# A delta-net inverse by substitution in blocks of four and two doublings, and product groups two steps apart

## The chip, the cores and the metric

The kernel runs on one core of a Trainium2 chip. The metric is the device time of one execution in microseconds (us), and lower is better. The engines are named as in the profile: PE is the matmul engine (PEld its weight loads, which overlap the matmuls), DVE the vector engine, ACT the scalar engine, POOL GpSimd, and SP the queue that issues most DMAs. L12 is line 12 of the kernel's file.

## The reference

One decoder layer runs on 512 prompt tokens and on 64 sample tokens (8 sequences of 8), 576 columns in all, with a model width of 2048. The layer is a normalisation, an input projection, eight gated delta-net heads beside four mLSTM heads, an output projection with a residual, and a convolutional FFN of width 5632. Everything is fp32. The part that the change touches is the solve in a delta-net head:

```python
lower = jnp.where(strict, jnp.einsum('nbhik,nbhjk->nbhij', kb, k) * decay, 0.0)
a_mat = lower + jnp.eye(c, dtype=lower.dtype)
solve = functools.partial(lax.linalg.triangular_solve, left_side=True, lower=True, unit_diagonal=True)
u = solve(a_mat, v * beta[..., None])
w = solve(a_mat, kb * jnp.exp(G)[..., None])
```

followed by a scan over chunks that carries a 128x128 state per head. For every chunk a unit triangular matrix has to be inverted, or something equal to it.

## The kernel before

**Dense work.** The large products (input projection, output projection, FFN) are done as three fp32r matmuls for each fp32 one: a weight tile is cut into a high and a low part (ACT makes the high part at L120, DVE the low part at L121), and so is the activation. `three` (L198) issues the six matmuls of one 128x128 weight tile, three kinds by two column halves of 288. I call these six a *step*. After each step `tick` (L170) runs the jobs that are due.

**Jobs.** A head is a Python generator, and `yield n` puts its next piece n steps later. So PE's order is written out by hand: dense steps, and between them the small products of the heads, in groups, where the yields put them. PE is the only engine with a hand-made order (`manual_schedule`, L274). For DVE, ACT, POOL and SP a scheduler makes the order from dependences and priorities, at build time. On the chip each engine runs its list in order; an instruction that waits holds back all behind it.

**PSUM.** The dense products use two buffers called `pd`; all small products take one of four buffers called `pr` in turn (`psr`, L111). A product that takes a buffer waits until the last reader of the product that had it four groups earlier is done.

**A delta-net head** (`dn_head`), 128 keys by 128 values, works on four chunks of 128 prompt tokens and one block of 64 sample tokens. Its groups on PE, in order: L608 (four transposes of k), the sample's products (L614 to L616), whose results feed the short DVE chain L619 to L628 that makes the scale factors `cj`; L635 (k by k, scaled on DVE by L638 into the matrix U); L646 (k by q, scaled by L647); L657 and L662 (transposes of v). Each yield between these groups is one step. Then come the inverse's own groups, the state chain over four chunks (L676, L683, L687, L690; L693 makes the new state on DVE), the sample's products as a job of their own (`dn_sample`, L747 to L771, with L774 on DVE updating the sample states), and a last normalisation over the head's output (L256). The next heads are computed beside this, so the late groups of one head stand among the early groups of the next.

**The inverse** (`inverse`) of a 128x128 unit triangular U starts with its 16x16 diagonal blocks. POOL masks them out, DVE folds them (L797 to L799) into `cb`, and two DMAs through DRAM (`ud`, L803 and L807) put the 40 blocks of a head on 40 partitions, each with its 256 elements along the free axis in the first part of the buffer T. DVE then negates (L809), sets the diagonal (L810) and does a back substitution in 14 pairs of an outer product (L815) and a subtraction (L817). Two DMAs (`xd`, L818, and `cx`, L821) bring the blocks back; L834 spreads them into a block-diagonal X and L836 transposes it into T. From there matmuls double the block size three times (16 to 32, 64, 128), beginning with L843; YI = 8 and YJ = 20 steps lie between the stages, in which the DMAs and the DVE chain run. The 28 instructions L815 and L817 and the DMA L818 have a higher priority (PQ = 1000) in the scheduler.

Of the kernel before, what the change touches and what calls it, by code (L numbers as in the profile page):

```python
# [11 lines left out]
ALU = mybir.AluOpType  # L12
# [20 lines left out]
SB = 16  # L33
# [35 lines left out]
class Layer:  # L69
# [515 lines left out]
    def dn_head(self, h, q, k, v, sz):  # L585
        nc, I, O = self.nc, self.I, self.O
        V, A, Pl, mm = nc.vector, nc.scalar, nc.gpsimd, nc.tensor.matmul
# [18 lines left out]
        for c in range(NCH):  # L606
            sl, n = self.blk(c)
            nc.tensor.transpose(pk[:, sl], k[:, sl], self.ident)  # L608
        for c in range(NCH):
            sl, n = self.blk(c)  # L610
# [15 lines left out]
        U, KQ = self.r(), em  # L626
        V.scalar_tensor_tensor(out=U[0:64, sl4], in0=pk[0:64, P:P + 64], scalar=cjc(4), in1=em[0:64, sl4], op0=ALU.mult, op1=ALU.mult)
        V.tensor_tensor(out=KQ[0:64, sl4], in0=pk[0:64, P + 64:2 * P], in1=em[0:64, sl4], op=ALU.mult)  # L628
        yield 1


        pr = self.psr()
        for c in range(NCH):
            sl, n = self.blk(c)
            mm(pr[:, sl], k[:, sl], k[:, sl], start=True, stop=True)  # L635
        for c in range(NCH):
            sl, n = self.blk(c)
# [1 line left out]
        res = []  # L639
        inv = self.inverse(U, res, YZ if h == 0 else 0)  # L640
        next(inv)
        yield 1
        pr = self.psr()
        for c in range(NCH):
            sl, n = self.blk(c)
            mm(pr[:, sl], k[:, sl], q[:, sl], start=True, stop=True)  # L646
        V.tensor_tensor(out=KQ[:, 0:SEQ], in0=pr, in1=em[:, 0:SEQ], op=ALU.mult)  # L647
        A.activation(q[:, 0:NT], q[:, 0:NT], AF.Square, scale=float(np.sqrt(EPS * P)))
        yield 1


        vs = self.r()
# [2 lines left out]
        for c in range(NCH):  # L655
            sl, n = self.blk(c)
            nc.tensor.transpose(pv[:, sl], v[:, sl], self.ident)  # L657
        for c in range(NCH):
            sl, n = self.blk(c)
# [7 lines left out]
        X, Xs = res  # L667
# [4 lines left out]
        for c in range(NCH):  # L672
            sl, n = self.blk(c)
# [24 lines left out]
            yield W  # L698
        self.later(4, O["pS"][h], S)
        while not sample[3]:  # L700
            yield 1


        ob, sq2 = qe, q[:, 0:NT]
        sq, rs_o, a, u = kd, vs, KQ, X
# [72 lines left out]
    def inverse(self, U, res, more):  # L778
# [3 lines left out]
        V, A, Pl, mm = nc.vector, nc.scalar, nc.gpsimd, nc.tensor.matmul  # L782
        c4 = lambda t: t[:, 0:SEQ].rearrange("p (c i) -> p c i", c=NCH)
        blocks = lambda t, n: t.rearrange("p (c b i) -> p c b i", c=n, i=SB)
        X, T = self.r(), self.r()
        d = lane = T
        Xs = self.t1([64, 64], "Xs", 2)
        nb = P // SB
# [5 lines left out]
        for t, o in ((blocks(d[:, 0:SEQ], NCH), cb[:, 0:4]), (blocks(d[0:64, SEQ:NT], 1), cb[0:64, 4:5])):  # L794
            n = t.shape[2]
            while n > 2:
# [4 lines left out]
        rows = lambda t: t.rearrange("c b r i -> (b r) c i")  # L801
        lanes = lambda t: t.rearrange("c b r i -> (c b) r i")
        nc.sync.dma_start(out=rows(ud), in_=cb)  # L803
        u, x = (lane[0:5 * nb, SB * SB * i:SB * SB * i + SB * SB].rearrange("p (r i) -> p r i", i=SB)
                for i in range(2))
        w = lane[0:5 * nb, 2 * SB * SB:2 * SB * SB + 4 * SB]
        nc.sync.dma_start(out=u, in_=lanes(ud))  # L807
        yield YI
        V.tensor_scalar(out=x, in0=u, scalar1=-1.0, scalar2=None, op0=ALU.mult)  # L809
        V.memset(lane[0:5 * nb, SB * SB:2 * SB * SB:SB + 1], 1.0)  # L810
        self.tc.cur_priority -= PQ
        for j in range(SB - 2, 0, -1):
            n = SB - 1 - j
            wv = w[:, 0:j * n].rearrange("p (r i) -> p r i", r=j)
            V.tensor_tensor(out=wv, in0=u[:, 0:j, j:j + 1].to_broadcast([5 * nb, j, n]),  # L815
                            in1=x[:, j:j + 1, j + 1:].to_broadcast([5 * nb, j, n]), op=ALU.mult)
            V.tensor_tensor(out=x[:, 0:j, j + 1:], in0=x[:, 0:j, j + 1:], in1=wv, op=ALU.subtract)  # L817
        nc.sync.dma_start(out=lanes(xd), in_=x)  # L818
        self.tc.cur_priority += PQ
        cx = self.t1([P, 5, SB], "cx", 2)  # L820
# [10 lines left out]
        for t, c, k in ((blocks(X[:, 0:SEQ], NCH), cx[:, 0:4], P), (blocks(Xs, 1), cx[0:64, 4:5], 64)):  # L831
            n = k // SB
            shape = list(t.shape)
            V.tensor_tensor(out=t, in0=c.unsqueeze(2).to_broadcast(shape),  # L834
                            in1=self.con[0:k, C_RB:C_RB + n].unsqueeze(1).unsqueeze(3).to_broadcast(shape), op=ALU.mult)
# [38 lines left out]
        for a in range(2):  # L874
            x = Xv[64 * a:64 * a + 32, :, 64 * a + 32:64 * a + 64]
# [6 lines left out]
        for c in range(NCH):  # L882
            o = c * CH
# [4 lines left out]
        for c in range(NCH):  # L888
            o = c * CH
            mm(pr[0:64, o + 64:o + CH], m[64:128, o:o + 64], X[64:128, o + 64:o + CH], start=True, stop=True)  # L890
        x = Xv[0:64, :, 64:128]
# [768 lines left out]
```

## Time and profile before

| what | value |
|---|---|
| median of 3 runs | 2695.42 us (2695.19 to 2695.53) |
| profiled execution | 2699.44 us |
| its span | 2697.7 us, PE clock 0.995 of full |
| PE busy | 2651.0 us (98%) |
| DVE busy | 1994.0 us (74%) |
| ACT busy | 1080.2 us (40%) |
| POOL busy | 333.6 us (12%) |
| DMA | 304.02 MB, mean 113 GB/s |

The profile is of one execution. A view by stretches gives each engine's busy time between two moments of the span, and the time that PE is not busy is the stretch less PE's number. A line of the view of waits reads: waiting engine, its tile and line, the tile and line that released it, total us, number of waits, longest. A line with a time in front is one instruction (or a run of the same): start in us from the span's start, duration in us, engine, line, operation, tiles, and in brackets the idle time before it with what ended it. A line of groups gives minimum, median and maximum, or busy time and mean.

### The profile page before, as it was taken

To read this page: it belongs to the slowest core of one execution; us is meant where nothing else is said; L and a number is where in the kernel's file an instruction comes from. 1 tells how busy PE (TensorE), PEld (TensorE's weight loads), DVE (VectorE), ACT (ScalarE), POOL (GpSimd) and SP (SyncE) were. 2 spreads that over 40 slices of the span, in tenths; PEclk is the share of its full clock that TensorE was granted. 3 is DMA by queue.
4 is the path that set the end of the run, shared out by engine and by line. 5 is a ranking of instruction groups with operands and counts; after the bars stand their busy time and mean duration, and the time that the engine had idled before them with its cause. 6 is when DMAs were issued, how large, how long until landed. Compare 5 with 4: busy or idle time off the path is not lost.

```text
span 2697.7 us, 48872 instructions
## 1 busy us (share of the span) xinstructions
PE 2651.0 (98%) x19967; PEld 2607.0 (97%) x19967; DVE 1994.0 (74%) x3338; ACT 1080.2 (40%) x1704; POOL 333.6 (12%) x658
## 2 busy tenths in 40 slices
PE   7999999999999999998999999999999999999998
PEld 7998999999999999998999999999999999999998
DVE  7887777765544332389888888888888888888646
ACT  5334344443333322254444444444444433433324
POOL 3222322222211001101000000000000100000001
PEclk9999999999999999999999999999999999999999
DMA  5222222222333344444333333333333373342333
GB/s 195 85 77 87 90 91 91 91 88 92 114 113 104 115 135 135 135 123 150 107 111 108 108 108 108 108 108 108 108 108 109 109 256 94 106 146 71 122 97 100
DMA packets 112233, 304.02 MB, mean 113 GB/s; under 512 B 21912, under 2 KB 28184, under 8 KB 112008
## 3 DMA queue, kind: packets, MB, share of 16 engines
q1 hardware_dynamic: 107896, 291.17, 34.0%
q0 software_dynamic: 1872, 7.37, 0.8%
q8 instruction: 156, 2.56, 0.4%
q10 hardware_dynamic: 2240, 2.36, 0.3%
q14 instruction: 69, 0.57, 0.1%
HBM read 264.79 MB, written 36.06 MB: 112 GB/s over the span
## 4 chain that ended last, share of the span: by engine, by line
PE 89%; DVE 4%; DMA 1%; issue 0%; ACT 0%; POOL 0%; DVEq 0%; POOLq 0%; SPq 0%; ACTq 0%
PE pd L198 36%; PE pr L1283 31%; PE pd L1283 12%; PE pr L198 3%; PE pr L1509 1%; DVE bl L121 1%; DVE wl L121 1%; DMA r<-hid 0%; DVE r L1544 0%; PE pr L256 0%; PE pr L843 0%; PE pr L980 0%; PE pr L982 0%; PE pr L690 0%; PE pr L687 0%
## 5 line engine op out<-in xcount | busy, mean ns | idle before, releaser
L120 ACT CAST wh<-raw 128x1024 fp32r<-128x1024 f32 (+1 forms) x394 | 404.6, 1027 | 741.1 <-PE pd L198 400.2
L1283 PE MATMUL pr<-bh,wh 128*128 128x288 f32 x2120 | 626.8, 296 | 1.9 <-ACT bh L120 1.9
L1283 PE MATMUL pr<-bh,wl 128*128 128x288 f32 x2120 | 624.6, 295 | 0.5 <-DVE wl L121 0.5
L1283 PE MATMUL pr<-bl,wh 128*128 128x288 f32 x2120 | 624.3, 294 | 0.6 <-DVE bl L121 0.6
L121 DVE TENSOR_TENSOR wl<-raw,wh 128x1024 fp32r<-128x1024 f32 (+1 forms) x394 | 476.5, 1210 | 178.8 <-ACT wh L120 172.4
L198 PE MATMUL pd<-ah,wh 128*128 128x288 f32 x2496 | 560.3, 306 | 0.0
L198 PE MATMUL pd<-ah,wl 128*128 128x288 f32 x2496 | 534.5, 296 | 0.2 <-DVE wl L121 0.2
L198 PE MATMUL pd<-al,wh 128*128 128x288 f32 x2496 | 533.8, 296 | 0.0
L198 PEld LDWEIGHTS pd<-ah,wh 128*128 128x128 f32 x2496 | 401.0, 189 | 14.2 <-issue 7.7
L198 PEld LDWEIGHTS pd<-ah,wl 128*128 128x128 f32 x2496 | 401.8, 189 | 0.5 <-DVE wl L121 0.5
L198 PEld LDWEIGHTS pd<-al,wh 128*128 128x128 f32 x2496 | 401.7, 189 | 0.0
L1283 PEld LDWEIGHTS pr<-bl,wh 128*128 128x128 f32 x2120 | 400.0, 189 | 1.1 <-DVE bl L121 1.1
L1283 PEld LDWEIGHTS pr<-bh,wh 128*128 128x128 f32 x2120 | 398.4, 188 | 2.1 <-ACT bh L120 2.1
L1283 PEld LDWEIGHTS pr<-bh,wl 128*128 128x128 f32 x2120 | 398.9, 188 | 1.2 <-DVE wl L121 1.2
L120 ACT CAST wh<-s 128x1024 fp32r<-128x1024 f32 (+1 forms) x171 | 169.6, 992 | 361.2 <-DVE s L1248 142.2
L1283 PE MATMUL pd<-bh,wh 128*128 128x288 f32 x848 | 252.2, 297 | 5.6 <-ACT wh L120 5.6
L1283 PE MATMUL pd<-bh,wl 128*128 128x288 f32 x848 | 250.8, 296 | 1.7 <-DVE wl L121 1.7
L1283 PE MATMUL pd<-bl,wh 128*128 128x288 f32 x848 | 249.7, 294 | 0.0
L121 DVE TENSOR_TENSOR wl<-s,wh 128x1024 fp32r<-128x1024 f32 (+1 forms) x171 | 196.5, 1149 | 26.0 <-ACT wh L120 18.4
L1283 PEld LDWEIGHTS pd<-bh,wh 128*128 128x128 f32 x848 | 160.3, 189 | 6.1 <-ACT wh L120 6.1
L1283 PEld LDWEIGHTS pd<-bh,wl 128*128 128x128 f32 x848 | 160.6, 189 | 2.2 <-DVE wl L121 2.2
L1283 PEld LDWEIGHTS pd<-bl,wh 128*128 128x128 f32 x848 | 161.0, 190 | 0.0
(400 smaller groups left out, 3501.1 us busy)
## 6 DMA issues: line engine op xcount, KB each, us to landing
raw<-in_w_up SPq DMA_DIRECT2D x176, 512.0 KB
raw<-in_w_in SPq DMA_DIRECT2D x114, 512.0 KB
raw<-in_w_down SPq DMA_DIRECT2D x40, 512.0 KB
raw<-in_w_out SPq DMA_DIRECT2D x32, 512.0 KB
raw<-in_w_down SPq DMA_DIRECT2D x40, 384.0 KB
hid<-r SPq DMA_DIRECT2D x44, 288.0 KB
r<-hid SPq DMA_DIRECT2D x40, 288.0 KB
r<-in_xT SPq DMA_DIRECT2D x32, 288.0 KB
```

The source lines that it names most:

```text
L120: nc.scalar.copy(hi, src)
L121: nc.vector.tensor_tensor(out=lo, in0=src, in1=hi.bitcast(F32), op=ALU.subtract)
L198: mm(outs[hf], w, x[:, hf * HALF:(hf + 1) * HALF], start=first and i == 0, stop=last and i == 2)
L1283: mm(out, w[:, ks], x[:, sl], start=k == 0 and i == 0, stop=k == nk - 1 and i == 2)
L1509: mm(pr[:, 0:n], w[:, ks], acts[kk][:, a * NT + sl.start:a * NT + sl.stop], start=kk == 0 and i == 0, stop=kk == FB - 1 and i == 2)
```

## The change

Three parts, all in the delta-net heads.

The 16x16 substitution is replaced. The four 4x4 blocks on the diagonal of each 16x16 block are solved together by substitution (two pairs of a multiplication, L823, and a subtraction, L824, on 8 elements per partition). Then block sizes double twice, 4 to 8 and 8 to 16: the off-diagonal part of the inverse is the product of three small matrices, computed on DVE as a broadcast multiplication into a scratch area (L834) and a sum along the last axis (L836, a TENSOR_REDUCE), twice for each doubling. Scratch is in the buffer X, which is filled only later; before, it was in T. The number of DVE instructions between the memset and the DMA is 16 in place of 28.

The three `yield 1` between a head's first groups (L629, L642, L649) become `yield 2`.

The poll `while not sample[3]: yield 1` (L701), by which a head waits for its sample job to end, becomes `yield 2`.

```diff
--- before.py
+++ after.py
@@ -626,7 +626,7 @@
         U, KQ = self.r(), em
         V.scalar_tensor_tensor(out=U[0:64, sl4], in0=pk[0:64, P:P + 64], scalar=cjc(4), in1=em[0:64, sl4], op0=ALU.mult, op1=ALU.mult)
         V.tensor_tensor(out=KQ[0:64, sl4], in0=pk[0:64, P + 64:2 * P], in1=em[0:64, sl4], op=ALU.mult)
-        yield 1
+        yield 2
 
 
         pr = self.psr()
@@ -639,14 +639,14 @@
         res = []
         inv = self.inverse(U, res, YZ if h == 0 else 0)
         next(inv)
-        yield 1
+        yield 2
         pr = self.psr()
         for c in range(NCH):
             sl, n = self.blk(c)
             mm(pr[:, sl], k[:, sl], q[:, sl], start=True, stop=True)
         V.tensor_tensor(out=KQ[:, 0:SEQ], in0=pr, in1=em[:, 0:SEQ], op=ALU.mult)
         A.activation(q[:, 0:NT], q[:, 0:NT], AF.Square, scale=float(np.sqrt(EPS * P)))
-        yield 1
+        yield 2
 
 
         vs = self.r()
@@ -698,7 +698,7 @@
             yield W
         self.later(4, O["pS"][h], S)
         while not sample[3]:
-            yield 1
+            yield 2
 
 
         ob, sq2 = qe, q[:, 0:NT]
@@ -801,20 +801,39 @@
         rows = lambda t: t.rearrange("c b r i -> (b r) c i")
         lanes = lambda t: t.rearrange("c b r i -> (c b) r i")
         nc.sync.dma_start(out=rows(ud), in_=cb)
-        u, x = (lane[0:5 * nb, SB * SB * i:SB * SB * i + SB * SB].rearrange("p (r i) -> p r i", i=SB)
-                for i in range(2))
-        w = lane[0:5 * nb, 2 * SB * SB:2 * SB * SB + 4 * SB]
+        L = 5 * nb
+        u, x = (lane[0:L, SB * SB * i:SB * SB * i + SB * SB].rearrange("p (r i) -> p r i", i=SB) for i in range(2))
         nc.sync.dma_start(out=u, in_=lanes(ud))
         yield YI
         V.tensor_scalar(out=x, in0=u, scalar1=-1.0, scalar2=None, op0=ALU.mult)
-        V.memset(lane[0:5 * nb, SB * SB:2 * SB * SB:SB + 1], 1.0)
+        V.memset(lane[0:L, SB * SB:2 * SB * SB:SB + 1], 1.0)
         self.tc.cur_priority -= PQ
-        for j in range(SB - 2, 0, -1):
-            n = SB - 1 - j
-            wv = w[:, 0:j * n].rearrange("p (r i) -> p r i", r=j)
-            V.tensor_tensor(out=wv, in0=u[:, 0:j, j:j + 1].to_broadcast([5 * nb, j, n]),
-                            in1=x[:, j:j + 1, j + 1:].to_broadcast([5 * nb, j, n]), op=ALU.mult)
-            V.tensor_tensor(out=x[:, 0:j, j + 1:], in0=x[:, 0:j, j + 1:], in1=wv, op=ALU.subtract)
+
+        def diag(o, n):
+
+            k = SB // n
+            t = lane[0:L, o:o + k * n * (SB + 1)].rearrange("p (b e) -> p b e", b=k)
+            return t[:, :, 0:n * SB].rearrange("p b (r i) -> p b r i", i=SB)[:, :, :, 0:n]
+
+
+        U4, X4 = diag(0, 4), diag(SB * SB, 4)
+        for j in (2, 1):
+            wv = X[0:L, 0:4 * j * (3 - j)].rearrange("p (b r i) -> p b r i", b=4, r=j)
+            full = list(wv.shape)
+            V.tensor_tensor(out=wv, in0=U4[:, :, 0:j, j:j + 1].to_broadcast(full), in1=X4[:, :, j:j + 1, j + 1:].to_broadcast(full), op=ALU.mult)
+            V.tensor_tensor(out=X4[:, :, 0:j, j + 1:], in0=X4[:, :, 0:j, j + 1:], in1=wv, op=ALU.subtract)
+
+        for n in (4, 8):
+            for b in range(SB // (2 * n)):
+                xb = diag(SB * SB, 2 * n)[:, b]
+                q = b * n * n * (n + 1)
+                tmp = X[0:L, q:q + n * n * n].rearrange("p (r i k) -> p r i k", r=n, i=n)
+                M = X[0:L, q + n * n * n:q + n * n * (n + 1)].rearrange("p (r i) -> p r i", i=n)
+                full = list(tmp.shape)
+                for o, l, r in ((M, xb[:, 0:n, n:2 * n], xb[:, n:2 * n, n:2 * n]), (xb[:, 0:n, n:2 * n], xb[:, 0:n, 0:n], M)):
+                    V.tensor_tensor(out=tmp, in0=l.unsqueeze(2).to_broadcast(full),
+                                    in1=r.rearrange("p k i -> p i k").unsqueeze(1).to_broadcast(full), op=ALU.mult)
+                    V.tensor_reduce(out=o, in_=tmp, axis=mybir.AxisListType.X, op=ALU.add)
         nc.sync.dma_start(out=lanes(xd), in_=x)
         self.tc.cur_priority += PQ
         cx = self.t1([P, 5, SB], "cx", 2)
```

From L818 on the new file's line numbers are 19 higher (L818 becomes L837, L843 becomes L862); in the text on the order, names are the program's: `pr` and `pd` are PSUM buffers, `r` any of the 128x576 buffers in SBUF, `wh` and `wl` weight parts, `ah` and `al` activation parts, `st` the sample states, `ss` and `cj` scale factors.

PE, in the third head (head 2, counted from 0), from its group L635 on; before:

```order
L635 MATMUL pr_2700<-r_2042 128x128 x4
L198 MATMUL pd_2740<-ah_123,wh_2457 128x288 x2
L198 MATMUL pd_2740<-al_124,wh_2457 128x288 x2
L198 MATMUL pd_2740<-ah_123,wl_2458 128x288 x2
L683 MATMUL pr_2753<-rr_2647,r_1773 128x128
L646 MATMUL pr_2756<-r_1847,r_2042 128x128 x4
L198 MATMUL pd_2740<-ah_121,wh_2457 128x288 x2
L198 MATMUL pd_2740<-al_122,wh_2457 128x288 x2
L198 MATMUL pd_2740<-ah_121,wl_2458 128x288 x2
L771 MATMUL pr_2769<-vm_2601,kp_2585 128x512
L657 MATMUL pr_2777<-con,r_2256 128x128 x4
L662 MATMUL pr_2786<-con,r_2256 64x128
```

The same place after:

```order
L635 MATMUL pr_2725<-r_2011 128x128 x4
L198 MATMUL pd_2648<-ah_115,wh_2424 128x288 x2
L198 MATMUL pd_2648<-al_116,wh_2424 128x288 x2
L198 MATMUL pd_2648<-ah_115,wl_2425 128x288 x2
L771 MATMUL pr_2756<-vm_2595,kp_2579 128x512
L198 MATMUL pd_2648<-ah_113,wh_2424 128x288 x2
L198 MATMUL pd_2648<-al_114,wh_2424 128x288 x2
L198 MATMUL pd_2648<-ah_113,wl_2425 128x288 x2
L646 MATMUL pr_2768<-r_1835,r_2011 128x128 x4
```

Two steps instead of one stand between L635 and L646, and another product of the sample job of head 1 (L771) stands between them in place of L683, so the four `pr` buffers go round in another order.

DVE, at head 2's start (L619 to L628 and L638), where L774 updates the sample states of the head before; before:

```order
L619 TENSOR_SCALAR ss_2661<-ss_2661 128x5
L622 RECIPROCAL ss_2661<-ss_2661 128x5
L623 TENSOR_TENSOR cj_2686<-ss_2661,cols 128x4
L624 TENSOR_TENSOR cj_2686<-ss_2661,cols 64x1
L638 SCALAR_TENSOR_TENSOR r_2691<-pr_2700,cj_2686,r_2540 128x128
L627 SCALAR_TENSOR_TENSOR r_2691<-pr_2678,cj_2686,r_2540 64x64
L638 SCALAR_TENSOR_TENSOR r_2691<-pr_2700,cj_2686,r_2540 128x128
L628 TENSOR_TENSOR r_2540<-pr_2678,r_2540 64x64
L638 SCALAR_TENSOR_TENSOR r_2691<-pr_2700,cj_2686,r_2540 128x128 x2
L798 TENSOR_TENSOR r_2710<-r_2710 64x32
L774 SCALAR_TENSOR_TENSOR st_1634<-st_1634,last_1649,pr_2769 128x128
L536 TENSOR_TENSOR r_2725<-pd_2454,rstd 128x288
```

After:

```order
L774 SCALAR_TENSOR_TENSOR st_1622<-st_1622,last_1637,pr_2756 128x128 x4
L619 TENSOR_SCALAR ss_2671<-ss_2671 128x5
L710 SCALAR_TENSOR_TENSOR r_1201<-r_1201,par,r_1413 128x576
L622 RECIPROCAL ss_2671<-ss_2671 128x5
L545 SCALAR_TENSOR_TENSOR r_2640<-r_2633,cwh,r_2640 128x600
L623 TENSOR_TENSOR cj_2696<-ss_2671,cols 128x4
L624 TENSOR_TENSOR cj_2696<-ss_2671,cols 64x1
L545 SCALAR_TENSOR_TENSOR r_2640<-r_2633,cwh,r_2640 128x600
L627 SCALAR_TENSOR_TENSOR r_2701<-pr_2688,cj_2696,r_2536 64x64
L693 SCALAR_TENSOR_TENSOR S_2786<-S_2613,last_1637,pr_2782 128x128
L628 TENSOR_TENSOR r_2536<-pr_2688,r_2536 64x64
L638 SCALAR_TENSOR_TENSOR r_2701<-pr_2725,cj_2696,r_2536 128x128 x3
```

The four L774, two steps of the convolution (L545), the end of an earlier head (L710) and a state update (L693) now stand among the instructions that make head 2's scale factors.

DVE, head 2's inverse; the first pairs of the substitution before:

```order
L809 TENSOR_SCALAR r_2710<-r_2710 40x256
L815 TENSOR_TENSOR r_2710<-r_2710 40x14
L810 MEMSET r_2710 40x16
L817 TENSOR_TENSOR r_2710<-r_2710 40x14
L815 TENSOR_TENSOR r_2710<-r_2710 40x26
L817 TENSOR_TENSOR r_2710<-r_2710 40x13x2
L815 TENSOR_TENSOR r_2710<-r_2710 40x36
L549 SCALAR_TENSOR_TENSOR r_2725<-r_2725,r_2732 128x512
L817 TENSOR_TENSOR r_2710<-r_2710 40x12x3
L551 SCALAR_TENSOR_TENSOR r_2725<-r_2725,r_2732 128x64
L815 TENSOR_TENSOR r_2710<-r_2710 40x44
L817 TENSOR_TENSOR r_2710<-r_2710 40x11x4
```

The two doublings after:

```order
L834 TENSOR_TENSOR r_2734<-r_2735 40x64 x2
L836 TENSOR_REDUCE r_2734<-r_2734 40x16 x2
L834 TENSOR_TENSOR r_2734<-r_2735,r_2734 40x64 x2
L836 TENSOR_REDUCE r_2735<-r_2734 40x4x4 x2
L545 SCALAR_TENSOR_TENSOR r_2908<-r_2901,cwh,r_2908 128x600
L834 TENSOR_TENSOR r_2734<-r_2735 40x512
L545 SCALAR_TENSOR_TENSOR r_2908<-r_2901,cwh,r_2908 128x600
L836 TENSOR_REDUCE r_2734<-r_2734 40x64
L121 TENSOR_TENSOR wl_2920<-raw_2917,wh_2919 128x1024
L834 TENSOR_TENSOR r_2734<-r_2735,r_2734 40x512
L545 SCALAR_TENSOR_TENSOR r_2908<-r_2901,cwh,r_2908 128x600
L836 TENSOR_REDUCE r_2735<-r_2734 40x8x8
```

Conv (L545) and weight work (L121) stand between the inverse's instructions in both programs, at other places.

## The prediction

> **What bounds the kernel now.** I read the page first: engine shares and the chain that ended last.
>
> ```profile
> span 2697.7 us, 48872 instructions
> PE 2651.0 (98%) x19967; PEld 2607.0 (97%) x19967; DVE 1994.0 (74%) x3338; ACT 1080.2 (40%) x1704; POOL 333.6 (12%) x658
> PE 89%; DVE 4%; DMA 1%; issue 0%; ACT 0%; POOL 0%; DVEq 0%; POOLq 0%; SPq 0%; ACTq 0%
> ```
>
> TensorE (PE) is the bound: 46.7 us of the span are all that it is not busy. The change adds and removes no matmul, so it can only move the part of those 46.7 us that lies where its instructions run, in the eight delta-net heads. The next view is the busy time by stretches of the heads' time.
>
> ```profile
> core 0: us, PE busy (x) PEld busy (x) DVE busy (x) ACT busy (x) POOL busy (x), PEclk, DMA share, GB/s
> 100.00:200.00 100.00, 98.96 (x775) 95.22 (x774) 76.94 (x201) 37.36 (x97) 34.09 (x47) 1.00 0.25 74
> 200.00:232.00 32.00, 32.00 (x258) 29.73 (x258) 17.64 (x37) 15.75 (x31) 8.38 (x8) 1.00 0.30 107
> 232.00:272.00 40.00, 34.28 (x256) 32.62 (x255) 35.97 (x93) 18.07 (x41) 11.60 (x19) 1.00 0.30 93
> 272.00:340.00 68.00, 67.62 (x534) 64.61 (x533) 48.89 (x122) 27.57 (x66) 23.97 (x29) 1.00 0.28 89
> 340.00:640.00 300.00, 298.72 (x2356) 284.81 (x2355) 209.32 (x505) 121.39 (x279) 80.21 (x109) 1.00 0.29 90
> ```
>
> PE idles 1.0, 0, 5.7, 0.4 and 1.3 us: 8.4 us in the 540 us of the heads, two thirds of it in 232 to 272 us, which is head 2 (counted from 0). There DVE is busy for 36 of 40 us. The granted clock is 1.00 throughout, so no part of this is the clock. What PE waits for is in the view of waits from 120 to 700 us:
>
> ```profile
> PE pr L843 <- DVE r L836: 3.1, 1, 3.1
> PE pr L657 <- DVE r L628: 1.9, 2, 1.5
> PE pr L771 <- DVE r L647: 1.0, 1, 1.0
> PE pr L646 <- ACT r L684: 0.6, 1, 0.6
> PE pr L662 <- DVE r L628: 0.6, 1, 0.6
> PE pr L1015 <- DVE hn L965: 0.5, 1, 0.5
> PE pr L687 <- ACT r L684: 0.5, 1, 0.5
> PE pr L866 <- DVE cb L799: 0.3, 1, 0.3
> ```
>
> L1015 belongs to an mLSTM head and stays. The other seven come to 8.0 us: 3.1 us behind the inverse (L836 is its last step before the first product, L843), the rest almost all waits for a PSUM buffer (pr has four) or an operand of neighbouring product groups. A group that starts late also pays its first weight load, so the pool is a little above the 8.4 us; I take 9.0. **The change can gain no more than about 9 us of 2695**, 0.33%. The question is how much of the 9 goes, and what comes new.
>
> **The change part by part.** *The inverse.* Before, 28 DVE instructions in one dependent chain (14 of L815, 14 of L817) follow a negation, L809. After, 16: four of 8 elements, eight of 64 or 16 in four independent pairs, four that read 512. Rows for the durations:
>
> ```profile
> L815 DVE TENSOR_TENSOR r<-r x112: 159/195/1332, 132.8 to 595.8; 40x14 f32<-40x14 f32 x16, 40x26 f32<-40x26 f32 x16, 40x36 f32<-40x36 f32 x16, 40x44 f32<-40x44 f32 x16
> L836 DVE STREAM_TRANSPOSE r<-r 128x512 f32<-128x512 f32 x8 | 5.6, 696 | 0.0
> L809 DVE TENSOR_SCALAR r<-r 40x256 f32<-40x256 f32 x8 | 4.6, 574 | 3.6 <-DMA r<-ud 3.6
> L545 DVE SCALAR_TENSOR_TENSOR r<-r,cwh,r 128x600 f32<-128x600 f32 x72 | 63.2, 877 | 1.2
> 254.45 1.47 POOL L707 TENSOR_TENSOR r<-r,r 128x576 f32<-128x576 f32 x1 [7.30 <-ACT r L706]
> 254.66 1.33 DVE L815 TENSOR_TENSOR r<-r 40x56 f32<-40x56 f32 x1
> 259.54 0.73 DVE L815 TENSOR_TENSOR r<-r 40x36 f32<-40x36 f32 x1
> 261.83 1.27 DVE L815 TENSOR_TENSOR r<-r 40x26 f32<-40x26 f32 x1
> ```
>
> With the median 0.195 us and some 0.03 us between dependent ones (264.19 + 0.17 to 264.39 below), 28 x 0.22 = 6.2 us, plus 0.35 for L809: 6.55 us of its own. After: four at the row's minimum, 0.16 + 0.03, are 0.8; a pair of independent 64-element ones about 0.4, four times 1.6; a 512-element one is taken as the 0.70 of L836, four times 0.72 = 2.9; with L809 5.6 us. No row shows a TENSOR_REDUCE: from below 512 elements cannot beat the fastest 256 ones, 0.28 (the row of 250.51 below), from above the 1.33 us of a blocked L815; I stay at 0.70, since L836 reads as many elements one after the other. So the chain alone saves 1 us, between 0.3 us lost and 1.8 us won for the two reductions. By itself that is little; what matters is what else stands in it.
>
> ```profile
> 232.40 0.60 PE L608 MATMUL pr<-con,r 128*128 128x128 f32 x4
> 240.41 0.21 DVE L628 TENSOR_TENSOR r<-pr,r 64x64 f32<-64x64 f32 x1
> 240.67 0.66 PE L657 MATMUL pr<-con,r 128*128 128x128 f32 x4 [1.49 <-DVE r L628]
> 244.76 0.21 DVE L799 TENSOR_TENSOR cb<-r 128x64 f32<-128x64 f32 x1
> 250.51 0.28 DVE L809 TENSOR_SCALAR r<-r 40x256 f32<-40x256 f32 x1
> 264.19 0.17 DVE L817 TENSOR_TENSOR r<-r 40x14 f32<-40x14 f32 x1
> 264.39 3.35 DMA xd<-r
> 267.75 1.94 DMA cx<-xd
> 271.21 1.16 PE L843 MATMUL pr<-r,r 128*128 128x128 f32 x8 [3.11 <-DVE r L836]
> ```
>
> In head 2 the inverse lasts from 250.51 to 264.36, 13.85 us: 6.55 of its own, 2.7 lost in the three long L815 (1.33 + 0.73 + 1.27 less three times 0.2; the first of them ends as POOL's L707 does, which started before it), and 4.6 for conv and weight work put between. In the new order L549, L551 and L693 no longer stand between, so at most 4.6 of that stays: 5.6 + 4.6 = 10.2 us, 3.6 us earlier, if no collision comes back.
>
> The Trainium skill (SBUF — State Buffer, Who interferes with whom) says that a DVE instruction with two SBUF inputs and a GpSimd one that reads SBUF exclude each other for a whole instruction, and that a reduction never does. The 1.33 us row agrees. By that rule 10 of the 16 new instructions are exposed instead of 28, so 2.7 x 10/28 = 1.0 us of collisions would remain (an estimate), the chain would be 11.2 us, and the time 1 us above my forecast. For the reduction the skill (VectorE: DVE Perf Modes, the perf-mode tier table) gives the 1x rate of an fp32 tensor_tensor, with which the sum stays.
>
> *The spacing.* A step (six 128x288 matmuls) lasts 0.80 us:
>
> ```profile
> 122.83 27.18 PE pd L198 x204
> ```
>
> 27.18 / 34 steps. The group of L635 now comes one step later, L646 two, L657 and all that follows in the head three: 2.4 us more for DVE, ACT and POOL at no cost in PE work, since in both orders as many steps lie between heads and from step 633 on PE's order is the same. A delayed head delays the head two behind it: heads 2 and 3 start at steps 226 and 282 (223 and 282 before), heads 4 to 7 where they did. Nothing runs uncovered at the end. On SP's queue the xd write still stands ahead of weight loads, and is ready earlier; PE waited for no weight load there before.
>
> *Head 2 after, from its L608.* Before, PE was free for L843 at 271.21 - 3.11 = 268.1, 35.7 us after L608, with some 3.1 us of stalls on the way (0.6 L646, 1.5 and 0.6 at L657/L662, 0.5 L687). Free of these 32.6, plus three steps: 35.0. The data came at 38.8. But DVE's new order is worse at the head's start: L619 stands behind the four L774 of a product that itself comes later, two L545 (0.88 each) stand before L627, and L693 before L628. So L628, which ended 8.2 us after L608, ends at about 10.5 by these rows (at least 8.2, at most 11.5). L657 waits for it in the new program; PE gets there at 240.67 - 1.49 - 0.6 = 238.6, 6.2 after L608, plus 2.4 and L687's group (some 0.5) moved ahead: 9.0. A stall of 1.5 stays, shared with L646. While DVE waits at L693 for PE, L628, the four L638, a weight split and L647 queue behind it. The inverse's data: 38.8 + 2.3 - 3.6 = 37.5 against 35.0 + 1.5 = 36.5: a stall of 1.0 instead of 3.1 (0 to 3.3).
>
> *Heads 4 to 7.* Head 7 lost the 1.0 us of the view of waits at L771, for the buffer that L647 reads; heads 4 to 6 only just made it. Head 4:
>
> ```profile
> 369.01 0.60 PE L608 MATMUL pr<-con,r 128*128 128x128 f32 x4
> 377.75 0.68 DVE L647 TENSOR_TENSOR r<-pr,r 128x512 f32<-128x512 f32 x1
> 378.57 0.47 PE L771 MATMUL pr<-vm,kp 96*128 96x512 f32 x1
> ```
>
> L647 ended 9.4 us after L608 and L771 starts 0.14 behind it. In the new program it is L676 that takes this buffer, two steps further: 9.4 + 1.6 = 11.0. L647 now stands behind L693 and two L724, about 10.0 by an estimate (each as long as L628's 0.21): covered by 1.0 us; I leave 0.3 over all four for a collision like those above. Heads 0, 1 and 3 had the remaining 0.7 us (L866's 0.3, 0.4 of L657's); I leave 0.2.
>
> **Sum.** 9.0 less what remains, 1.5 + 1.0 + 0.3 + 0.2 = 3.0: **6.0 us gained**. The profiled execution took 2699.44 us, 1.7 more than its span; with the change it would be 2693.4. The median of the runs, 2695.42, is 4.0 below it; the same 6.0 us makes **2689.4**. 0.2% is 5.4 us (about what a measurement of this kernel can tell from no change), so a gain at this edge.
>
> **Rivals.** *Everything goes*: the new order of DVE at head 2 costs nothing, since PE itself arrives later there. Gain 8.4 to 9.8, about 2686.0. For it: DVE is idle 4 of 40 us even there. Against: L619's new place.
> *Head 2 stays late*: collisions come back in full (2.7) and L628 ends at 11.5; stalls of 2.5 and 3.3 remain. Gain 9.0 - 6.3 = 2.7: 2692.7. For it: POOL works 11.6 us in that stretch. This is also the case in which the shorter inverse does not do what it says, because its own time falls by 1 us only.
> *Slower*: PSUM buffers. In heads 3 to 7 the next product after L647 reuses its buffer; L647's queue now holds L693, which waits for PE, and L724. It decides at 11.0 us after L608. Should L647 end at 14 us, five heads lose 3.0 each, 15.0 us, and the time is 2695.4 - 9.0 + 3.0 + 15.0 = 2704.4; at 13.0 it would be 2699.4. Against: in head 4's rows it ended at 9.4.
>
> **How the numbers follow.** Forecast 45% (its own range 2687.5 to 2691.5; 38 of the 45 below 2690.0), everything goes 15%, head 2 stays late 34%, slower 6%. Faster by over 0.2%: 38 + 15 = 53%; within: 7 + 34 = 41%; slower 6%. The range reaches from 2685.6, where all 9.8 us go, to 2696.2, where the gain is lost and a little more.
>
> **What would show it.** Right: PE idle from 232 to 275 us falls from 5.7 to about 2.5; the wait of head 2's first inverse product (L862 in the new file) is about 1 us, that of L657 about 1.5; the L771 waits vanish; inverse of head 2 near 10 us; DVE's busy time falls by 5 to 10 us. Wrong: waits of L676 or L764 for L647 or L628 in heads 4 to 7; a TENSOR_REDUCE of 512 elements above 1 us; PE waiting for a weight split; any change of PE's idle time after 680 us.

## The result: slower by 1%

| | before | changed |
|---|---|---|
| median of five runs | 2695.53 us (2695.19 to 2697.49) | 2721.96 us (2721.46 to 2723.54) |
| ratio | 1 | 1.0098, 95% interval 1.0084 to 1.0113 |
| profiled execution, span | 2699.44 us, 2697.7 us | 2721.46 us, 2719.7 us |

The change costs 26.4 us. Forecast were 2689.4 us and a range of 2685.6 to 2696.2, so the time lies on the other side and far outside. No rival reached it.

The first lines of the changed kernel's page, with the engine shares, and its chain:

```profile
span 2719.7 us, 48799 instructions
PE 2659.3 (98%) x19967; PEld 2613.6 (96%) x19967; DVE 2003.2 (74%) x3242; ACT 1079.7 (40%) x1704; POOL 329.5 (12%) x658
PE 82%; DVE 9%; issue 2%; DMA 2%; ACT 1%; POOL 1%; DVEq 0%; SPq 0%; POOLq 0%; ACTq 0%
```

PE is still busy for 98% of the span, with the same number of instructions, but DVE's share of the chain that ended last went from 4% to 9%. PE's busy time itself rose by 8.3 us (2651.0 to 2659.3) with nothing more to do. That rise is a part of the loss, as the clock below shows.

Where it went is seen in the stretches of the heads' time. The view of the changed kernel:

```profile
core 0: us, PE busy (x) PEld busy (x) DVE busy (x) ACT busy (x) POOL busy (x), PEclk, DMA share, GB/s
100.00:200.00 100.00, 97.19 (x753) 94.22 (x752) 72.15 (x170) 36.77 (x95) 32.28 (x44) 0.98 0.25 76
...
232.00:272.00 40.00, 37.51 (x283) 36.50 (x283) 34.80 (x80) 20.52 (x45) 12.55 (x17) 1.00 0.30 93
272.00:340.00 68.00, 62.37 (x480) 59.14 (x479) 52.52 (x110) 23.92 (x61) 23.15 (x31) 0.97 0.26 83
340.00:640.00 300.00, 286.13 (x2193) 270.73 (x2193) 213.60 (x443) 115.58 (x267) 72.17 (x100) 0.99 0.26 84
```

From 100 to 640 us PE now idles 24.8 us instead of 8.4, over half of it (13.9 instead of 1.3) in 340 to 640 us, the heads that the prediction gave 0.3 us. What PE waits for from 100 to 700 us, in the changed kernel:

```profile
PE pr L683 <- DVE rr L678: 5.5, 4, 1.5
PE pr L885 <- DVE r L876: 4.6, 4, 2.8
PE pr L662 <- ACT r L696: 3.9, 4, 1.9
PE pr L862 <- POOL r L869: 3.3, 1, 3.3
PE pr L256 <- POOL r L707: 2.5, 3, 1.6
PE pr L657 <- DVE r L628: 1.9, 1, 1.9
PE pr L676 <- DVE r L647: 1.4, 1, 1.4
PE pr L676 <- DVE S L693: 1.1, 2, 0.8
PE pr L646 <- DVE ss L619: 0.6, 1, 0.6
```

The one wait of 3.1 us for the inverse has become 21 waits at eight places of the heads: the state chain (L676, L683), the inverse's second level (L885), the last normalisation (L256), the transposes of v (L657, L662), and still the inverse's first product (L862, in head 2).

The second part is the clock. Two stretches of the changed kernel after waits, and one of the kernel before after its wait of 3.1 us:

```profile
276.00:279.00 3.00, 3.00 (x14) 3.00 (x15) 2.96 (x3) 0.59 (x1) 3.00 (x2) 0.50 0.18 71
604.00:610.00 6.00, 5.58 (x23) 5.49 (x24) 5.23 (x21) 0.87 (x4) 0.00 (x0) 0.50 0.38 101
```

```profile
271.20:275.20 4.00, 3.99 (x32) 3.99 (x33) 3.47 (x8) 1.61 (x2) 3.10 (x3) 1.00 0.05 20
```

The column ahead of the last two is the granted clock: 0.50 for 3 and for 6 us, in which PE is busy but does half of its work. Read in shorter stretches, the clock was at 0.50 from 163.3 to 166.7, from 275.9 to 279.3 and from 603.6 to 610.4 us, 13.7 us in all. PE was busy for 12.8 of them, so this cost some 6.4 us. Before, there was none between 100 and 700 us. The sum: 24.8 - 8.4 of waits and 6.4 of clock are 22.8 us.

The heads' time as a whole can be measured from head 0's first transpose to the last state product of the first mLSTM head. Its end before, and after:

```profile
674.66 0.59 PE L982 MATMUL pr<-st,r 128*128 128x257 f32 x2
```

```profile
695.55 0.59 PE L1001 MATMUL pr<-st,r 128*128 128x257 f32 x2
```

It begins with head 0's L608 at 116.08 us before and at 113.48 after, so it lasts 558.6 us before and 582.1 after: 23.5 us more, which the 22.8 nearly explain. The spans of the two profiled executions differ by 22.0 us: 23.5 more in the heads, 2.6 less ahead of them and 1.1 more behind. The 26.4 us are a difference of medians. The profiled execution before took 3.9 us more than the median, the one after 0.5 us less. Why single executions differ so I did not follow.

### The profile page after: what moved, and what is told of

It reads as the page before. It is cut to its first block, busy times and chain, and to the rows that moved or that the text cites. A ratio compares the mean times of both kernels' runs of the same rounds, so it can differ in the third digit from the quotient of the medians.

```text
span 2719.7 us, 48799 instructions
## 1 busy us (share of the span) xinstructions
PE 2659.3 (98%) x19967; PEld 2613.6 (96%) x19967; DVE 2003.2 (74%) x3242; ACT 1079.7 (40%) x1704; POOL 329.5 (12%) x658
## 4 chain that ended last, share of the span: by engine, by line
PE 82%; DVE 9%; issue 2%; DMA 2%; ACT 1%; POOL 1%; DVEq 0%; SPq 0%; POOLq 0%; ACTq 0%
PE pr L1302 31%; PE pd L198 30%; PE pd L1302 12%; PE pr L198 3%; PE pr L1528 1%; DVE wl L121 1%; DVE r L545 1%; DVE r L834 1%; DVE bl L121 1%; DMA r<-hid 0%; DVE r L798 0%; DVE vp L724 0%; DVE r L1563 0%; POOL irk L621 0%; DMA ud<-cb 0%
## 5 line engine op out<-in xcount | busy, mean ns | idle before, releaser
L121 DVE TENSOR_TENSOR wl<-raw,wh 128x1024 fp32r<-128x1024 f32 (+1 forms) x394 | 475.0, 1206 | 169.0 <-ACT wh L120 162.7
L121 DVE TENSOR_TENSOR wl<-s,wh 128x1024 fp32r<-128x1024 f32 (+1 forms) x171 | 196.5, 1149 | 26.1 <-ACT wh L120 18.6
```

The source lines that it names most:

```text
L121: nc.vector.tensor_tensor(out=lo, in0=src, in1=hi.bitcast(F32), op=ALU.subtract)
```

## The experiments

In the table each run is compared with runs of the kernel before on the same chip in the same session. The heads' time and PE's idle time (100 to 640 us, from the view of stretches) are each from one profiled execution, read as above. They agree with the ratios to within some 4 us only: h2_old_12 is 0.6 us shorter in the heads and, by its ratio, 3.5 us slower.

| run | inverse | spacing and what else | ratio, 95% interval | heads' time against before, us | PE idle, us |
|---|---|---|---|---|---|
| before | old | old | 1 | 0 | 8.4 |
| changed kernel | new | new | 1.0098, 1.0084 to 1.0113 | +23.5 | 24.8 |
| inv_only | new | old | 1.0054, 1.0039 to 1.0069 | +15.1 | 16.9 |
| gaps_poll | old | new | 1.0114, 1.0097 to 1.0131 | +28.3 | 28.7 |
| inv_poll | new | only the poll | 1.0052, 1.0037 to 1.0066 | +15.0 | 16.7 |
| inv_gaps | new | all but the poll | 1.0087, 1.0072 to 1.0102 | +24.0 | 25.2 |
| inv_urgent | new | old, L678 urgent | 1.0011, 1.0002 to 1.0020 | +1.4 | 8.7 |
| after_urgent | new | new, L678 urgent | 1.0079, 1.0066 to 1.0093 | +19.6 | 22.4 |
| gaps_back | old | new, later groups back | 1.0021, 1.0012 to 1.0030 | +6.4 | 13.6 |
| after_back | new | new, later groups back | 1.0033, 1.0020 to 1.0046 | +9.5 | 14.8 |
| tail_late | old | old, later groups 3 steps on | 1.0104, 1.0089 to 1.0120 | +27.6 | 26.9 |
| before_h2 | old | old, head 2's six steps on | 1.0012, 1.0003 to 1.0021 | +2.5 | 9.1 |
| h2_old_12 | old | as gaps_back, head 2's twelve on | 1.0013, 1.0004 to 1.0021 | -0.6 | 7.5 |
| h2_new_12 | new | as after_back, head 2's twelve on | 1.0005, 0.9996 to 1.0014 | -1.2 | 6.2 |
| after_list | new | new, all chains urgent | 1.0041, 1.0027 to 1.0054 | +7.2 | 15.1 |
| h2_new_list | new | as h2_new_12, all chains urgent | 1.0002, 0.9993 to 1.0011 | -3.5 | 5.0 |

### Which part costs it

Three theories: A, the inverse's long instructions stand ahead of the state chain on DVE; B, the spacing moves the groups; C, only both together. The first four runs put the two parts (and the poll) apart. The first is the changed kernel with the four yields as they were:

```diff
-        yield 2
+        yield 1
```

(L629, L642, L649 and, in the poll, L701).

> The new inverse with the old spacing (the three group yields and the poll at one step). Theory A, the inverse's six 512-element instructions stand ahead of the state chain and cost PE its waits: most of the 26 us stay, 2715 to 2722, waits of L683 for L678 above 1 us in heads 4 to 6. Theory B, the spacing does it: 2691 to 2697, no wait of L683, L676 or L256. Theory C, only both together: 2691 to 2699.

Measured: 2713.55 us, 1.0054. The second is the kernel before with the four yields at two:

```diff
-        yield 1
+        yield 2
```

> The old inverse with the new spacing (all four yields at two steps). Theory A: 2691 to 2697, no waits in heads 4 to 7. Theory B: 2715 to 2722 with the waits of L676, L683, L662 and L256 as in the changed kernel. Theory C: 2691 to 2699.

Measured: 2729.7 us, 1.0114. The other two put back the poll's yield or the three group yields in the changed kernel:

> The new inverse and the poll of two steps, the three group yields at one. If the poll makes L256 wait (2.5 us in the changed kernel), that wait stays here and the time is 2 to 4 us above the new inverse alone; if the group yields do it, the wait is gone and the time is that of the new inverse alone within 2 us.

> The new inverse and the three group yields of two steps, the poll at one. If the group yields carry the loss (theory B or C), 2716 to 2722, with all waits but L256's 2.5 us; if the poll carries it, 2691 to 2700.

Measured: 1.0052 and 1.0087. The poll does nothing (1.0052 beside 1.0054, 1.0087 beside the changed kernel's 1.0098; with the poll at one, L256 waits 2.4 us instead of 2.5). A and B are each right about half (A's run came out 1.5 us below its range, B's 7.7 us above it), and C is wrong: either part alone makes the kernel slower, the spacing alone by more than both together. Had they added, the changed kernel would have lost 15.1 + 28.3 us in the heads, and it lost 23.5. So neither part has a cost of its own that simply adds. The waits of the two runs differ in place, too. The new inverse alone:

```profile
PE pr L683 <- DVE rr L678: 9.2, 3, 3.2
```

The new spacing alone:

```profile
PE pr L843 <- DVE r L836: 9.4, 1, 9.4
PE pr L866 <- DVE r L857: 8.5, 3, 2.8
```

The first has one large new wait, once in each of the heads 4, 5 and 6, of 3.0 to 3.2 us with half a clock behind it; head 2's wait of 3.1 us for the inverse, the prediction's main term, is gone. The second waits for the inverse's second level, and in head 2 for its first product longer than ever.

### The new inverse: L678's place in DVE's list

In head 4 of the new inverse alone, by the time line (PE's L676, the last three rows of DVE before its result, PE's L683):

```profile
383.31 0.38 PE L676 MATMUL pr<-S,r 128*128 128x128 f32 x2
```

```profile
386.56 1.20 DVE L121 TENSOR_TENSOR wl<-raw,wh 128x1024 fp32r<-128x1024 f32 x1
387.70 1.00 DVE L834 TENSOR_TENSOR r<-r 40x512 f32<-40x512 f32 x1
388.62 0.33 DVE L678 SCALAR_TENSOR_TENSOR rr<-pr,cols,r 128x128 f32<-128x128 f32 x1
```

```profile
389.10 0.71 PE L683 MATMUL pr<-rr,r 128*128 128x128 f32 x2 [3.03 <-DVE rr L678]
```

L678's operand was there at 383.7. It started at 388.62, because it stands in DVE's list behind two convolution steps, the inverse's small products, a weight split and the first of its multiplications of 512. DVE was never idle in between. In the kernel before the same pair stood well:

```profile
388.96 0.38 PE L683 MATMUL pr<-rr,r 128*128 128x128 f32 x2
```

```profile
388.07 0.34 DVE L678 SCALAR_TENSOR_TENSOR rr<-pr,cols,r 128x128 f32<-128x128 f32 x1
```

It ended 0.55 us before PE wanted it. Two theories: D, only the place in the list does it; E, DVE has too much to do here and the wait moves on. The test makes L678 urgent and changes nothing else:

```diff
+                self.tc.cur_priority -= 2000
                 V.scalar_tensor_tensor(out=rr, in0=pr[:, 0:P], scalar=self.col(1, c, 1, h), in1=vs[:, sl], op0=ALU.mult, op1=ALU.add)
+                self.tc.cur_priority += 2000
```

> The new inverse, old spacing, and one priority: L678 (the operand of L683) is made more urgent than the inverse, which moves it in DVE's list ahead of a weight split and five entries of the inverse, 3.7 us of work by the rows of the new inverse alone; nothing else of the program's work changes. Theory D, only the place in DVE's list made PE wait: the three waits of L683 (3.0 to 3.2 us each) and the reduced clock behind them go, 15 us less than the new inverse alone, 0.9985 to 1.0005 of before. Rival E, the inverse is too much work for DVE at this place and the wait moves to the next instruction behind it (L853, L875): at most 5 us less, 1.003 to 1.006 of before, with a wait of L862 or L885 above 1 us in heads 4 to 6.

> The changed kernel with L678 made urgent. Theory D: the four waits of L683 (5.5 us) go, the others stay: 4 to 7 us below the changed kernel, 1.006 to 1.008 of before. Rival E: the waits move on, no gain beyond 2 us.

With the new inverse alone the ratio fell from 1.0054 to 1.0011, PE's idle time from 16.9 to 8.7 us, and no half clock was left in the heads: D. The gain against before that I expected beside it (0.9985 to 1.0005) did not come, since the 3.1 us won in head 2 came back as new small waits: L657 in head 1, 1.4 us, the second product of the inverse (L874 in the changed kernel) in heads 4 to 6, 1.2 us together, and others of 0.3 to 0.7. In the changed kernel the same edit brought the ratio to 1.0079, 5 us less and inside the 4 to 7 expected (the heads' time fell by 3.9 us, from 23.5 to 19.6 above before). L683's wait fell from 5.5 to 1.0 us, and two others rose: L885's from 4.6 to 5.3, L256's from 2.5 to 3.3.

### The spacing: three steps put the inverse's second level behind the evictions

L856 subtracts the first level's product and L857 transposes the result, which L866 on PE takes. Head 4 before, on DVE and then PE:

```profile
408.68 0.67 DVE L856 TENSOR_TENSOR r<-r,pr 128x512 f32<-128x512 f32 x1
409.38 0.71 DVE L857 STREAM_TRANSPOSE r<-r 128x512 f32<-128x512 f32 x1
410.31 0.46 DVE L536 TENSOR_TENSOR r<-pd,rstd 128x288 f32<-128x288 f32 x1 [0.21 <-PE pd L198]
```

```profile
411.00 0.68 PE L866 MATMUL pr<-r,r 128*64 128x64 f32 x8
```

The same with the new spacing, DVE, POOL and PE:

```profile
422.54 0.45 DVE L536 TENSOR_TENSOR r<-pd,rstd 128x288 f32<-128x288 f32 x1
...
423.33 1.88 DVE L121 TENSOR_TENSOR wl<-raw,wh 128x1024 fp32r<-128x1024 f32 x1
425.13 0.68 DVE L856 TENSOR_TENSOR r<-r,pr 128x512 f32<-128x512 f32 x1
...
426.17 0.70 DVE L857 STREAM_TRANSPOSE r<-r 128x512 f32<-128x512 f32 x1
```

```profile
422.70 1.42 POOL L711 TENSOR_TENSOR r<-r,r 128x576 f32<-128x576 f32 x1 [4.53 <-DVE r L710]
424.07 1.21 POOL L540 COPY dnst<-r 128x27 f32<-128x27 f32 x1
```

```profile
427.02 0.65 PE L866 MATMUL pr<-r,r 128*64 128x64 f32 x8 [2.84 <-DVE r L857]
```

A dense tile takes 16 steps, and its evictions (L536 to L538) and a weight split come at a fixed place of them. Before, L857 had just ended when the tile was done. Three steps later, L856 and L857 stand behind that block in the list (L855 on PE, whose result L856 takes, had ended at 421.0), and the weight split in it takes 1.88 us where it took 1.2 elsewhere, with POOL at work beside it. In the changed kernel the rows of head 4 are the same: a split of 1.87 us at 417.56, then L875, which is L856 there; L885 on PE waited 0.6 us. Theory F: only the later groups' place against the dense tiles counts. Rival G: the late product groups L635 and L646 cost it by themselves. Three runs: the later groups three steps earlier again, with the new spacing and either inverse,

```diff
-        yield YI
+        yield YI - 3
         yield from inv
```

> The old inverse, the new spacing, and the yield ahead of the inverse's first product (L665) three steps shorter, so that all groups behind it stand where they stood before. Theory F, the three steps moved the inverse's products against the dense tiles, so that L856 and L857 came to stand behind the evictions L536 to L538: the three waits of L866 (2.8 us) and those of L662 go, within 0.3% of before, except where head 2's inverse has now less time (its wait of L843 3 to 6 us): 1.000 to 1.004. Rival G, the late L635 and L646 themselves cost it (L619 behind the sample's updates, buffers): most of the loss stays, 1.008 to 1.012.

> The changed kernel with the yield at L665 three steps shorter. Theories D and F together: it is like the new inverse alone, 1.004 to 1.007 of before, with L683 waiting for L678 in heads 4 to 6 and no waits of L256, L676 and L662 above 1 us in heads 4 to 6. Rival G: 1.008 to 1.012.

and the kernel before with that one yield three longer:

```diff
-        yield YI
+        yield YI + 3
         yield from inv
```

> The kernel before with one number changed: the yield ahead of the inverse's first product (L665) is 11 steps instead of 8, the gaps between the product groups stay at one step. Theory F (only the place of the later groups against the dense tiles counts): the three waits of L866 (2.8 us) of heads 4 to 6 and the reduced clock behind them appear as with the new spacing, 12 to 20 us slower, 1.0045 to 1.0075. Rival G (the gaps between L635, L646 and L657 cost it): within 0.2% of before, or faster, since head 2's wait of 3.1 us has 2.4 us more.

One number in the kernel before, no operation added or moved between engines, makes it 27.6 us slower in the heads (1.0104), about what the new spacing cost (28.3) and more than I expected. L866 waits 1.7 to 1.8 us in each of the heads 4 to 6 instead of 2.8: in head 4, L856 started at 428.32, behind L536 to L538 and a split of 1.88 us. More waits stand beside it than with the new spacing (L843 7.9 us in two), the longest of them in heads 0 and 2, where the theory had named none. The first three:

```profile
PE pr L866 <- DVE r L857: 5.2, 3, 1.8
PE pr L662 <- DVE r L628: 4.8, 2, 4.2
PE pr L676 <- DVE S L693: 4.5, 4, 2.0
```

And with the later groups back in their places the spacing's loss shrinks from 1.0114 to 1.0021, and the changed kernel's from 1.0098 to 1.0033. From 340 to 640 us PE then idles 0.17 us with the old inverse, less than the 1.3 us before. G falls, and F holds in this: the place of the later groups makes most of the loss. That they stand badly against the dense tiles, and not against the groups of other heads, was followed only for the waits of L866 (8.5 of the 28.7 us with the new spacing) and is not shown for the rest. What was left is nearly all in head 2: L843 waits 10.6 us there (expected were 3 to 6), and the clock was at 0.50 from 266.9 to 280.5 us, within the wait and for 5.1 us behind it; with the new inverse L862 waits 8.6 us. L683, which I had expected to wait in after_back as with the new inverse alone, did so for 0.3 us at most, and the ratio came out below the 1.004 to 1.007 expected: its place had moved as well.

### Head 2 and a version that might win

If head 2 lacks time, twelve steps more ahead of its first inverse product should give it:

```diff
-        yield YI
+        yield YI - 3 + (12 if h == 2 else 0)
```

> The old inverse, the new spacing, the later groups back in their old places (as in the run that took the yield at L665 three steps shorter), but in head 2 alone twelve steps more ahead of the inverse's first product. If head 2's wait of 10.6 us with the reduced clock behind it is all that was left, it goes: PE idle of the heads 3 to 4 us against 8.4 before, 4 to 7 us faster than before, 0.9975 to 0.9990. If the wait moves on with the groups (L853's like stands behind the evictions at the new place), 1.000 to 1.003.

> The changed kernel with the later groups back in their old places and twelve steps more in head 2. If head 2's wait of 8.6 us was all that was left: 1 to 5 us faster than before, 0.9980 to 1.0000. If the new inverse itself costs (waits of L676, L683, L885 of some 4 us in all stay): 1.000 to 1.002.

```diff
-        yield YI
+        yield YI + (6 if h == 2 else 0)
```

> The kernel before with six steps more ahead of the inverse's first product in head 2 alone. The prediction's pool: its wait of 3.1 us goes and nothing comes, 2 to 4 us faster, 0.9985 to 0.9993. If the moved groups fall behind other work of DVE, as the later groups of the new spacing did: 1.000 to 1.004.

Only h2_new_12 lost its wait, and it comes out level (1.0005, 0.9996 to 1.0014). The other two still wait at the moved place, 5.5 us twelve steps (9.6 us) later in h2_old_12, and in the kernel before 3.5 us six steps later, where 3.1 had been. Why is seen on DVE in head 2 of before_h2 (L834 spreads the blocks that the DMA brought, in two parts):

```profile
266.54 0.22 DVE L834 TENSOR_TENSOR Xs<-cx,con 64x64 f32<-64x64 f32 x1 [1.51 <-DMA cx<-xd]
...
269.01 1.87 DVE L121 TENSOR_TENSOR wl<-raw,wh 128x1024 fp32r<-128x1024 f32 x1
...
271.25 1.20 DVE L834 TENSOR_TENSOR r<-cx,con 128x512 f32<-128x512 f32 x1
```

The data were there at 266.5 us, 4.8 us before PE came for them (at 271.4, where its wait of 3.5 began). The large part of L834 began at 271.25, behind a normalisation, the evictions and a weight split. The yield gave time, and the list that was made with it gave the time away. In the kernel before itself the blocks did come late: L834 waited for the DMA until 269.72 us, 1.6 us after PE was free, and L834 and L836 took most of the other 1.5. There the wait was a lack of time, as the prediction had counted it; given the time, it became a matter of the list.

### Order or place

Open was then whether in the changed kernel itself priorities can mend the lists while PE's list stays. The run makes every DVE and ACT instruction between two groups of a head urgent, in the form of the edit to L678:

> The changed kernel, with every DVE and ACT instruction between two product groups of a head (scale factors, L638, L647, L678, L684, L693, L696, L853 to L911) made more urgent than all else in the scheduler; PE's list is that of the changed kernel. If priorities alone cure the waits, PE idle of the heads falls from 24.8 us to under 12 and the time to 1.001 to 1.004 of before. If the waits follow from where the groups stand against the dense tiles (the evictions L536 to L538 are ready first and a priority does not pass them), L885, L662, L862, L676 stay and only L683's 5.5 us goes: 1.006 to 1.009.

> The changed kernel with the later groups in their old places, twelve steps more in head 2, and the same urgency. The run without the urgency has 6 us of PE idle left in the heads. If the list's order makes these, 2 to 4 us faster than before, 0.9985 to 0.9995; if not, 1.000 to 1.001.

With PE's list unchanged, the ratio falls from 1.0098 to 1.0041: over half of the changed kernel's loss is the order of the lists. (The lines of this kernel are higher by its edit: L917 is L885, L692 is L676, L662 is L647, L907 is L876.)

```profile
PE pr L917 <- DVE r L907: 4.0, 4, 2.0
PE pr L692 <- DVE r L662: 3.2, 4, 1.7
```

What stays is of the other kind. L885 waits for L876 in spite of the urgency, since in heads 4 to 6 the evictions L536 to L538 still stand ahead of L875 in the list (0.7 us in each; its 2.0 us in head 0 came without them). So the run lies between my two cases: PE's idle time is 15.1 us, where one expected under 12 and the other that L885, L662, L862 and L676 go on waiting. L662's and L256's waits went, L862's and L683's shrank (to 1.6 and 1.4 us), L885's and L676's grew (to 6.4 and 3.2).

h2_new_list has the least idle time of all, 5.0 us, and 3.5 us less in the heads than before. Its time is level all the same, 1.0002 (0.9993 to 1.0011). The 3.5 us are outside what the interval allows (1.9 us faster). They compare one execution with one: this one took 2696.10 us, the shortest of its eleven, and that of the kernel before 2699.44, 3.9 above its median. No version here beats the kernel before by what can be measured.

## Why the prediction was wrong

**The bound was right and was read as a ceiling on both sides.** PE is the bound, no matmul came or went, and the pool of 9 us is what the change could gain. The mistake was to treat the other 530 us of the heads, in which PE did not wait, as nearly safe. There the lists of DVE and PE just met: L678 ended 0.55 us, L857 0.9 us ahead of PE. The prediction quoted such a case itself (L647 in head 4 ended 0.14 us ahead of L771) and moved to a loss of 0.3 us for all four heads.

**The step that failed: the spacing** "at no cost in PE work". It was costed as free time for DVE because as many steps lie between heads. But the later groups moved by three steps against the dense tiles, and that alone, in the kernel before, costs 27.6 us (tail_late). The comparison of DVE's lists was made at head 2's start and in its inverse; in heads 4 to 6, which repeat, L856 and L857 (L875 and L876 in the changed kernel) had gone behind L536 to L538, which no part of the prediction looked at.

**A second step failed: the new inverse** was priced by its own time in head 2, and what its long instructions do to the state chain's place in DVE's list was put at nothing. Alone it costs 15.1 us in the heads (inv_only), and 1.4 with L678 moved ahead of them (inv_urgent). Its rows, after:

```profile
L836 DVE TENSOR_REDUCE r<-r 40x64 f32<-40x512 f32 x16 | 10.8, 677 | 0.1
L834 DVE TENSOR_TENSOR r<-r,r 40x512 f32<-40x512 f32 x8 | 9.0, 1119 | 0.0
L834 DVE TENSOR_TENSOR r<-r 40x512 f32<-40x512 f32 x8 | 8.3, 1041 | 0.0
```

The reduction of 512 took 0.68 us (0.70 taken). The two multiplications of 512 took 1.04 and 1.12 instead of 0.70. The chain's own time is then, by an estimate, 5.6 + 0.8 = 6.4 us against 6.55 before: no gain of 1 us, and hardly a part of the loss. The loss came from where such pieces stand: L678 behind one of them.

**Head 2**, in the changed kernel:

```profile
234.65 0.60 PE L608 MATMUL pr<-con,r 128*128 128x128 f32 x4
275.90 1.41 PE L862 MATMUL pr<-r,r 128*128 128x128 f32 x5 [3.27 <-POOL r L869]
```

```profile
246.38 0.21 DVE L628 TENSOR_TENSOR r<-pr,r 64x64 f32<-64x64 f32 x1
256.32 0.28 DVE L808 TENSOR_SCALAR r<-r 40x256 f32<-40x256 f32 x1
267.58 0.73 DVE L836 TENSOR_REDUCE r<-r 40x64 f32<-40x512 f32 x1
273.82 0.69 DVE L853 TENSOR_TENSOR r<-cx,con 128x512 f32<-128x512 f32 x1
```

L628 ended 11.9 us after L608 (10.5 forecast, 11.5 at most), the inverse took 12.0 us (10.2), its product waited 3.3 us (1.0), and L646 and L657 waited 2.5 together (1.5). That is the rival "head 2 stays late" (2.5 and 3.3), which would have been 2692.7. Two collisions are in the 12.0 us, which the forecast's sum had left out: the first L823 took 1.29 us and the first L824 0.95, with POOL's L707 and L844 beside them, where the second of each took 0.15. And L853, which spreads the blocks, stands behind the evictions and a weight split: the DMA `cx` was issued at 269.85, and with the 1.94 us that it took before, an estimate, the blocks were there at 271.8. One reading in the working was off: L662's 0.6 us, counted among head 2's stalls, is in head 0 (at 122.56 us), so the forecast's wait of L862 would have been 0.5 instead of 1.0. Head 2 was mis-sized by 3.3 us, and beside the point: three quarters of the waits are elsewhere.

**The rival "slower"** had the right kind, L647 late on DVE, and a small share. In head 7 it ended 15 us after L608 and PE's L676 waited 1.4 us for it. In head 4 it ended 12.4 us after L608, past the 11.0 from which it was to decide, but PE came no earlier either. So one wait of the five it counted came, and no head lost 3 us. The two L724 ahead of L647, taken as 0.21 us each, took 1.19 and 1.10 in head 7, with POOL's L790 and L731 beside them.

**The clock** was left out. The forecast found 1.00 throughout and took it as given. 6.4 of the 23.5 us are half clock behind three waits. The page of the Trainium skill on the clock (TensorE: Matmul & The Clock Gate, What's actually happening) says that PE falls to half rate after an idle window of about 3.4 us, which runs freely. The traces agree on the half rate and on its length, 3.4 us or twice that. They do not agree on the threshold as a length of the wait: 2.8 us was enough at 159.8 us of the changed kernel, 3.1 us was not in the kernel before, and of three waits of 1.75 us in tail_late one was enough. With it, a forecast of waits of 3 us each should have carried about 1.7 us more for each that meets the gate.

Right were: the waits of L771 vanish, the reduction below 1 us, no wait for a weight split in the heads, PE's waits after 700 us nearly unchanged (11.0 us before, 11.3 after). Wrong, beside the above: DVE's busy time rose by 9 us instead of falling by 5 to 10, and PE's idle time from 232 to 275 us fell to 4.9 instead of 2.5 us.

## What to carry to other kernels

In a kernel whose bound engine is 98% busy and whose other lists are made at build time, a change of spacing is not slack given to anyone: it makes new lists, and every pair of a result and its consumer that only just met before is at stake. So before a forecast, compare the lists in the part that repeats most, find for each consumer on the bound engine what its producer now stands behind, and price that by the durations of the trace. Then test with one number: here a yield of three steps more, in the old kernel, showed in one run what the whole change did.

## What the runs showed of the hardware

- PE's granted clock fell to 0.50 behind some waits, for 3.4 or 6.8 us (13.7 us where a wait of 10.6 us lies within it, gaps_back), and whether it does depends on more than the wait's length. Waits of 2.8 and 3.0 us brought it (changed kernel; all three in inv_only), one of 3.1 us did not (before), of three of 1.75 us in tail_late only the one in head 4 did, and in head 7 of the changed kernel it came during a wait of 1.4 us that followed one of 1.9.
- A multiplication of 512 elements per partition with both operands broadcast and one transposed took 1.04 to 1.12 us, where the reduction of 512 took 0.68 and L647, which multiplies 512 in plain order with one operand in PSUM, 0.68.
- A weight split L121 took 1.21 us alone and 1.88 where POOL works beside it (L711 and L540 in the rows above); the one of 1.87 in before_h2 stands beside the same two. A split at the critical place is then 0.7 us later than its mean says.
